# The attention norm's factors spread by a matrix product of ones with a diagonal; the multiply on VectorE; squares moved ahead, sums of logs behind

## The chip, the core and the metric

The kernel runs on one core of one Trainium2 chip. A core has five engines that each work through their own instructions in order: TensorE (PE, matrix products into the eight banks of PSUM), VectorE (DVE), ScalarE (ACT), GpSimd (POOL) and SyncE (SP), which issues most of the transfers (DMAs) between DRAM and the on-chip memory SBUF. Engines wait for each other through semaphores. The metric is the device time of one execution in microseconds (us); lower is better.

## The reference, cut to what matters

Two layers over 512 tokens of width 1024: a mixer (forgetting attention in layer 0, a gated short convolution in layer 1), a squared-ReLU MLP and a gated embedding, each between RMS norms. The change lies in the first norm and in the projections of the attention:

```python
def rmsnorm(x, g):
    xf = x.astype(jnp.float32)
    y = xf * lax.rsqrt(jnp.mean(xf * xf, axis=-1, keepdims=True) + RMS_EPS)
    return (y * g.astype(jnp.float32)).astype(x.dtype)

hn = rmsnorm(x, g[0])
proj = hn @ w_in                              # q, k, v and a forget logit for each head
f_logit = (proj[..., 3 * D:] + b_f).astype(jnp.float32)
log_f = jax.nn.log_sigmoid(f_logit)
c = lax.cumsum(log_f, axis=1).transpose(0, 2, 1)
s = s + cb[..., :, None] - c[..., None, :]    # in each block of queries, before the softmax
```

Each token has one factor `r = rsqrt(mean(x*x) + eps)`. Each attention score gets a difference of running sums of the logs.

## The kernel before

**Numbers.** Each operand of a product is split in two parts, `hi` (cast by ScalarE, L276 or L285) and `lo` (the rest, by VectorE, L277 or L287), and `mm3` (L266 to L272) makes three products out of them. The weights pass through the same split, after they landed in one of 14 buffers `raw`; the gain `g` goes into the weights.

**Tokens and the two ways of the norm.** The tokens are four blocks of 128, `t` = 0 to 3. The input is also there transposed, channels on partitions, in two pages for each block (`raw_x[t][n]`, `xT` in the trace). The value projection comes in three chunks of columns. Chunk 0 (256 values and the 16 forget logits) and chunk 1 (512 values) are multiplied with the transposed input *without* the norm, and `r`, a number for each token and thus for each partition of the result, is applied to the result (`keep_values`, L491: `logit` at L496, ScalarE's `v` at L512, VectorE's at L517). Chunk 2 (256 values) and all `q`, `k` need the normed input, `hT`, whose tokens run along the free dimension. For that `r` must stand on all partitions as a row.

**The row of factors.** `mean_squares` (L701) sums the squares of a block on ScalarE and VectorE, `inverse` (L708) raises to -1/2 on GpSimd: `rs[t]`, one number for each partition. `rows_of` (L716) writes these 128 numbers to DRAM (`r_T`, L717) and reads them back broadcast to all partitions (`r_row`, L718), both on SP's queue. `normed_x` (L722) multiplies each page `xT` by that row on GpSimd (L726) and splits it into `hTh`, `hTl` (L277).

**The logs.** `logs` (L419) makes `log_sigmoid` of the logits of all blocks, with `logf` (L436) as its last step, split into `lf_h`, `lf_l`. `sums_of_logs` (L441) multiplies them with a triangle of ones (`ps_c`, L445), copies the bank (`c_T`, L450), makes `neg_c` (L454) and writes it to DRAM (L458). `bias` (L556) reads `neg_c` back, broadcast (`pr`, `prr`, `prl`, L568). `project` (L528) makes `q` and `k` of two heads; copies of `kh`, `kl` to the other half of the partitions go as transfers on SP (L553). `scores` (L574) multiplies them (`sc`, L581, L582) and adds the bias.

**What sets the order.** From L731 on, until the squares and chunk 0 are done, instructions stand on each engine as the code is written. Behind that, a scheduler places each engine's instructions by its own model of the times; a change there moves rows. SP's transfers use eight semaphores in turn, so each waits for the eighth before it; a weight load also waits until its `raw` buffer has been split.

Of the kernel before, what the change touches and what calls it, by code (L numbers as in the profile page):

```python
# [8 lines left out]
F32 = mybir.dt.float32  # L9
F32R = mybir.dt.float32r  # L10
AF = mybir.ActivationFunctionType
ALU = mybir.AluOpType
# [3 lines left out]
P = 128  # L16
# [5 lines left out]
KT = D // P  # L22
NB = S // P
# [6 lines left out]
RAWS = 14  # L30
# [38 lines left out]
def trunk(ctx: ExitStack, tc, x, xT, pT, g, gT, wv, wqk, bf, wo, wci, wcq, cw, wco, wup, wdn, wpp, wpg, out):  # L69
    nc = tc.nc  # L70
# [7 lines left out]
    dram = pool("dram", 1, space=DRAM)  # L78

    def page(name, dtype=F32):  # L80
        return pages.tile([P, S], dtype, tag="pg", name=name)

    def bank(name):
        return psum.tile([P, S], F32, tag="ps", name=name)
# [4 lines left out]
    ident = consts.tile([P, P], F32, tag="ident", name="ident")  # L89
# [322 lines left out]
    def attention(hT, raw_x, first_x, b_f, work, by_hand):  # L412
# [47 lines left out]
        turned, rs = {}, {}  # L460
# [237 lines left out]
        name = "n0"  # L698
        E = mybir.EngineType

        def mean_squares(t):  # L701
            half = lambda n: first_x[t][n][:, :S]
            q = squares(half(0), f"{name}_q0_{t}"), products(half(1), f"{name}_q1_{t}")
            v = stat(f"{name}_v{t}")
            nc.vector.tensor_tensor(out=v, in0=q[0], in1=q[1], op=ALU.add)
            return v

        def inverse(t, v):  # L708
            r = stat(f"{name}_r{t}")
            nc.gpsimd.tensor_tensor(out=r, in0=v, in1=neg_half, op=ALU.pow)  # L710
            return r

        r_T = dram.tile([NB, P], F32, tag="r_T", name="r_T")
        r_row = page("r_row")

        def rows_of(t):  # L716
            nc.sync.dma_start(r_T[t : t + 1, :].rearrange("o p -> p o"), rs[t])  # L717
            nc.sync.dma_start(  # L718
                r_row[:, t * P : (t + 1) * P], r_T[t : t + 1, :].partition_broadcast(P)
            )  # L720

        def normed_x(t):  # L722
            for n in range(2):
                h = raw_x[t][n][:, :S].rearrange("p (j c) -> p j c", j=4)
                r = r_row[:, t * P : (t + 1) * P].unsqueeze(1).to_broadcast([P, 4, P])
                nc.gpsimd.tensor_tensor(out=h, in0=h, in1=r, op=ALU.mult)  # L726
                to = lambda u: u[:, 4 * n : 4 * n + 4, t * P : (t + 1) * P]
                split(to(hT.hi), to(hT.lo), h)

        banks_v = [bank(f"v0_{t}") for t in range(NB)]  # L730
        with tc.manual_schedule(engines={E.PE, E.DVE, E.Activation, E.Pool}):  # L731
            work(9)
            split_x(0, 0)
            prepare(4)
            part(banks_v[0], 0, 0)
            split_x(0, 1)
            split_x(1, 0)
            part(banks_v[1], 1, 0)
            prepare(KT)
            part(banks_v[0], 0, 1)  # L740
            split_x(1, 1)
            part(banks_v[1], 1, 1)
            for t in (2, 3):
                for n in range(2):
                    split_x(t, n)
                    part(banks_v[t], t, n)
            for t in range(2):
                rs[t] = inverse(t, mean_squares(t))
                prepare(KT + 2 * t + 2)
            prepare(2 * KT)  # L750
            for t in range(2):
                keep_values(0, t, banks_v[t])
            for t in (2, 3):
                rs[t] = inverse(t, mean_squares(t))
                keep_values(0, t, banks_v[t])
        for t in range(NB):
            rows_of(t)
        tri = page("tri", F32R)
        ones = page("ones")
        nc.gpsimd.memset(ones[:, :S], 1.0)  # L760
# [5 lines left out]
        logs()  # L766
        for t in range(NB):
            values(1, t)
            normed_x(t)
            if t == 2:  # L770
                sums_of_logs(tri)
        bias(0)
        bias(1)
        for t in range(NB):
# [522 lines left out]
```

## Time and profile before

| | |
|---|---|
| median of three runs | 1241.15 us (1239.37 to 1241.65) |
| the profiled execution | 1239.36 us |
| its span, first to last instruction | 1237.6 us |
| busy in the span | PE 98%, VectorE 76%, ScalarE 56%, GpSimd 54% |
| DRAM traffic over the span | 118 GB/s |

Rows of the waits name who waited, for whom, the us in total, the number of waits and the longest. Rows of the timelines give start, length, engine, line, operation, output <- inputs, shapes, and in brackets the idle time before and what ended it; `x4` are four instructions merged in one row. A product of PE is issued when the one before it has streamed, so the distance of starts counts, not the length that is shown. SPq rows are issues of transfers, not their landing.

### The profile page before, as it was taken

Reading aid. Unit: us, or ns where it says so; the run is one execution under the profiler, and the core shown is the slowest. Engines: PE = TensorE matmul, PEld = TensorE weight load, DVE = VectorE, ACT = ScalarE, POOL = GpSimd, SP = SyncE. Lnnn points to the kernel's source line nnn. Section 1 sums busy time; section 2 is a strip of 40 time slices with the busy share of each in tenths; the row PEclk is TensorE's granted clock in tenths of the full one; section 3 lists DMA queues with packets and bytes.
Section 4 is the critical chain, followed back from the end, with each engine's and each line's share of the span. In section 5 each row is a group of like instructions: output and inputs, shape, how many; then the busy total and the mean of one; then the engine's idle time right before and its main releaser. Section 6 shows DMA issues by size and latency. Waiting matters only on the chain.

```text
span 1237.6 us, 18749 instructions
## 1 busy us (share of the span) xinstructions
PE 1208.8 (98%) x6167; PEld 1028.7 (83%) x6167; DVE 935.5 (76%) x1466; ACT 690.0 (56%) x1465; POOL 668.8 (54%) x620
## 2 busy tenths in 40 slices
PE   9589999999999999999999999999999999999997
PEld 7478888788888888888889999989888888888886
DVE  6677888776786778769867798867776887669873
ACT  5646787656745634564467443455756345635551
POOL 0426666426776877776213155415678777778310
PEclk9799999999999999999999999999999999999999
DMA  9364656261442244228332233443322442235501
GB/s 309 102 180 146 167 152 160 88 226 52 136 130 68 78 134 136 86 69 272 119 103 66 63 102 103 145 146 111 115 73 85 137 135 88 60 127 161 180 6 62
DMA packets 88465, 151.09 MB, mean 122 GB/s; under 512 B 10992, under 2 KB 19232, under 8 KB 88368
## 3 DMA queue, kind: packets, MB, share of 16 engines
q1 hardware_dynamic: 87792, 149.37, 38.9%
q8 instruction: 48, 0.79, 0.3%
q10 hardware_dynamic: 576, 0.53, 0.1%
q14 instruction: 49, 0.40, 0.1%
HBM read 139.29 MB, written 6.38 MB: 118 GB/s over the span
## 4 chain that ended last, share of the span: by engine, by line
PE 85%; DMA 5%; DVE 4%; issue 2%; ACT 2%; POOL 1%; SPq 0%; POOLq 0%; DVEq 0%; ACTq 0%
PE up L270 9%; PE up L269 9%; PE up L268 9%; PE dn L268 8%; PE dn L269 8%; PE dn L270 8%; PE qk L270 2%; PE qk L269 2%; PE qk L268 2%; PE pg L269 2%; PE pg L268 2%; PE pg L270 2%; DMA raw<-in_wqk 2%; PE pT L597 1%; PE co L269 1%
## 5 line engine op out<-in xcount | busy, mean ns | idle before, releaser
L277 DVE TENSOR_TENSOR wl<-raw,wh 128x512 fp32r<-128x512 f32 x346 | 349.2, 1054 | 14.3 <-ACT wh L276 13.5
L269 PE MATMUL up<-hTh,wl 128*128 128x512 f32 (+1 forms) x576 | 210.2, 365 | 0.0
L270 PE MATMUL up<-hTl,wh 128*128 128x512 f32 (+1 forms) x576 | 209.7, 366 | 0.1
L268 PE MATMUL up<-hTh,wh 128*128 128x512 f32 (+1 forms) x576 | 208.7, 366 | 0.0
L276 ACT CAST wh<-raw 128x512 fp32r<-128x512 f32 x346 | 189.4, 625 | 4.5 <-DVE xd L373 4.4
L949 ACT ACTIVATE r<-up 128x512 f32<-128x512 f32 (+1 forms) x72 | 39.4, 548 | 201.9 <-PE up L270 160.0
L277 POOL TENSOR_TENSOR wl<-dn_T,wh 128x512 fp32r<-128x512 f32 x96 | 132.2, 1410 | 30.1 <-ACT wh L276 30.1
L168 POOL TENSOR_TENSOR dn_T<-raw,raw 128x512 f32<-128x512 f32 x56 | 86.1, 1550 | 70.8 <-DMA raw<-in_wdn 55.5
L268 PEld LDWEIGHTS up<-hTh,wh 128*128 128x128 f32 x576 | 108.6, 189 | 17.6
L269 PEld LDWEIGHTS up<-hTh,wl 128*128 128x128 f32 x576 | 108.6, 189 | 17.5
L270 PEld LDWEIGHTS up<-hTl,wh 128*128 128x128 f32 x576 | 108.3, 189 | 17.7 <-DVE hTl L277 0.3
L995 DVE TENSOR_TENSOR acc<-dn,acc 128x512 f32<-128x512 f32 x168 | 107.5, 680 | 13.9 <-PE dn L270 13.9
L168 POOL TENSOR_TENSOR dn_T<-raw,dn_T 128x512 f32<-128x512 f32 x56 | 92.9, 1658 | 2.2
L276 ACT CAST wh<-dn_T 128x512 fp32r<-128x512 f32 x112 | 61.4, 617 | 11.0 <-POOL dn_T L168 11.0
L277 DVE TENSOR_TENSOR A12l<-q,A12h 128x512 fp32r<-128x512 f32 x28 | 22.5, 802 | 52.9 <-ACT A12h L276 52.9
L1009 POOL TENSOR_TENSOR acc<-acc,acc 128x512 f32<-128x512 f32 x28 | 46.9, 1709 | 9.9 <-DVE acc L995 9.9
L268 PE MATMUL qk<-hTh,wh 128*128 128x512 f32 x128 | 51.1, 400 | 0.0
L269 PE MATMUL qk<-hTh,wl 128*128 128x512 f32 x128 | 51.1, 399 | 0.0
L270 PE MATMUL qk<-hTl,wh 128*128 128x512 f32 x128 | 51.0, 398 | 0.0
L269 PE MATMUL pg<-wh,hTl 128*128 128x512 f32 x128 | 50.5, 394 | 0.0
L287 DVE SCALAR_TENSOR_TENSOR wl<-raw,first_g,wh 128x256 fp32r<-128x256 f32 (+2 forms) x88 | 46.1, 571 | 5.7 <-ACT wh L285 5.4
L268 PE MATMUL pg<-wh,hTh 128*128 128x512 f32 x128 | 50.4, 394 | 0.0
(409 smaller groups left out, 3310.3 us busy)
## 6 DMA issues: line engine op xcount, KB each, us to landing
raw<-in_wup SPq DMA_DIRECT2D x128, 256.0 KB, 3.0
raw<-in_wdn SPq DMA_DIRECT2D x128, 256.0 KB, 2.8
raw<-in_wcq SPq DMA_DIRECT2D x36, 256.0 KB, 2.8
raw<-in_wqk SPq DMA_DIRECT2D x32, 256.0 KB, 5.5
raw<-in_wpg SPq DMA_DIRECT2D x32, 256.0 KB, 4.4
g<-in_g SPq DMA_DIRECT2D x22, 256.0 KB, 5.9
prl<-neg_c SPq DMA_DIRECT2D x16, 256.0 KB, 6.2
raw<-in_wo SPq DMA_DIRECT2D x16, 256.0 KB, 4.8
```

The source lines that it names most:

```text
L168: ins = nc.gpsimd.tensor_tensor(out=B[name], in0=B[a], in1=B[b], op=op)
L268: nc.tensor.matmul(ps, a.hi, b.hi, start=start, stop=False)
L269: nc.tensor.matmul(ps, a.lo, b.hi, start=False, stop=False)
L270: nc.tensor.matmul(ps, a.hi, b.lo, start=False, stop=stop)
L276: nc.scalar.copy(hi, src)
L277: return eng.tensor_tensor(out=lo, in0=src, in1=hi.bitcast(F32), op=ALU.subtract)
L287: eng.scalar_tensor_tensor(out=lo[:, c], in0=src[:, c], scalar=first_g[:, k : k + 1], in1=hi[:, c].bitcast(F32), op0=ALU.mult, op1=ALU.sub ...
L597: nc.tensor.transpose(ps[:, b * P : (b + 1) * P], probs[h][b][:, j * P : (j + 1) * P], ident)
L949: nc.scalar.activation(r[:, :n], ps[:, :n], AF.Relu)
L995: ins = nc.vector.tensor_tensor(out=a, in0=banks[s], in1=a, op=ALU.add)
L1009: nc.gpsimd.tensor_tensor(out=a, in0=a, in1=acc[i, s][:, :S], op=ALU.add)
```

## The change

- The round trip through DRAM goes. `rows_of` makes a diagonal matrix of the factors on GpSimd (`r_d`, 128 x 128) and multiplies a matrix of ones with it on PE, so that a quarter of one PSUM bank, `r_rows`, holds the row on all partitions.
- `normed_x` multiplies on VectorE, from that bank.
- The squares of blocks 2 and 3 are taken before the last two weights of chunk 1 and before chunk 0's results are kept.
- In the loop over the blocks of chunk 1 the rows come in pairs, `normed_x` lags one block, and `sums_of_logs` stands behind the loop.

```diff
-        r_T = dram.tile([NB, P], F32, tag="r_T", name="r_T")
-        r_row = page("r_row")
+        all_ones = page("all_ones")
+        nc.gpsimd.memset(all_ones[:, :P], 1.0)
+        r_rows = []
 
         def rows_of(t):
-            nc.sync.dma_start(r_T[t : t + 1, :].rearrange("o p -> p o"), rs[t])
-            nc.sync.dma_start(
-                r_row[:, t * P : (t + 1) * P], r_T[t : t + 1, :].partition_broadcast(P)
+            if not r_rows:
+                r_rows.append(bank("r_rows"))
+            d = page(f"r_d{t}")
+            nc.gpsimd.tensor_scalar(
+                out=d[:, :P], in0=ident, scalar1=rs[t], scalar2=None, op0=ALU.mult
+            )
+            nc.tensor.matmul(
+                r_rows[0][:, t * P : (t + 1) * P], all_ones[:, :P], d[:, :P],
+                start=True, stop=True,
             )
 
         def normed_x(t):
             for n in range(2):
                 h = raw_x[t][n][:, :S].rearrange("p (j c) -> p j c", j=4)
-                r = r_row[:, t * P : (t + 1) * P].unsqueeze(1).to_broadcast([P, 4, P])
-                nc.gpsimd.tensor_tensor(out=h, in0=h, in1=r, op=ALU.mult)
+                r = r_rows[0][:, t * P : (t + 1) * P].unsqueeze(1).to_broadcast([P, 4, P])
+                nc.vector.tensor_tensor(out=h, in0=h, in1=r, op=ALU.mult)
                 to = lambda u: u[:, 4 * n : 4 * n + 4, t * P : (t + 1) * P]
                 split(to(hT.hi), to(hT.lo), h)
...
                 prepare(KT + 2 * t + 2)
-            prepare(2 * KT)
-            for t in range(2):
-                keep_values(0, t, banks_v[t])
+            prepare(RAWS)
             for t in (2, 3):
                 rs[t] = inverse(t, mean_squares(t))
+            prepare(2 * KT)
+            for t in range(NB):
                 keep_values(0, t, banks_v[t])
-        for t in range(NB):
-            rows_of(t)
...
         for t in range(NB):
             values(1, t)
-            normed_x(t)
-            if t == 2:
-                sums_of_logs(tri)
+            if t in (0, 2):
+                rows_of(t)
+                rows_of(t + 1)
+            if t:
+                normed_x(t - 1)
+        sums_of_logs(tri)
+        normed_x(3)
```

Where the instructions stand now, at three places. Lines of the changed kernel are up to nine higher behind the diff; L733 is the multiply of `normed_x`, L724 the product with the diagonal.

VectorE at the end of the logs (`wl` are weight halves, `f_l` and `logf` the logs). Before:

```order
L287 SCALAR_TENSOR_TENSOR wl_479<-raw_480,first_g,wh_478 128x256
L434 TENSOR_TENSOR f_l<-f_l,f_r 128x64
L287 SCALAR_TENSOR_TENSOR wl_479<-raw_480,first_g,wh_478 128x256
L277 TENSOR_TENSOR hTl<-xT_0_90,hTh 128x4x128
L436 SCALAR_TENSOR_TENSOR logf<-logit,f_l 128x64
L287 SCALAR_TENSOR_TENSOR wl_490<-raw_491,first_g,wh_489 128x256 x2
```

Now:

```order
L287 SCALAR_TENSOR_TENSOR wl_471<-raw_472,first_g,wh_470 128x256 x2
L434 TENSOR_TENSOR f_l<-f_l,f_r 128x64
L287 SCALAR_TENSOR_TENSOR wl_482<-raw_483,first_g,wh_481 128x256 x2
L436 SCALAR_TENSOR_TENSOR logf<-logit,f_l 128x64
L287 SCALAR_TENSOR_TENSOR wl_493<-raw_494,first_g,wh_492 128x256 x2
L287 SCALAR_TENSOR_TENSOR wl_504<-raw_505,first_g,wh_503 128x256 x2
```

No half of `hT` stands ahead of `logf` any more; the first one comes 12 rows behind it.

VectorE from the copy of the running sums, `c_T`, to `neg_c`. Before:

```order
L277 TENSOR_TENSOR hTl<-xT_0_96,hTh 128x4x128
L450 COPY c_T<-ps_c 16x512
L517 SCALAR_TENSOR_TENSOR v_0_555<-v_0_466,n_r_344,v_0_555 128x2x64 x2
L517 SCALAR_TENSOR_TENSOR v_1_556<-v_0_466,n_r_344,v_1_556 128x2x64 x2
L517 SCALAR_TENSOR_TENSOR v_0_596<-v_1_571,n_r_361,v_0_596 128x2x64 x2
L517 SCALAR_TENSOR_TENSOR v_1_597<-v_1_571,n_r_361,v_1_597 128x2x64 x2
L454 TENSOR_SCALAR neg_c_664<-c_T 16x128
```

Now:

```order
L733 TENSOR_TENSOR xT_1_97<-xT_1_97,r_rows 128x512
L517 SCALAR_TENSOR_TENSOR v_0_677<-v_3_652,n_r_395,v_0_677 128x2x64 x2
L517 SCALAR_TENSOR_TENSOR v_1_678<-v_3_652,n_r_395,v_1_678 128x2x64 x2
L450 COPY c_T<-ps_c 16x512
L277 TENSOR_TENSOR hTl<-xT_0_92,hTh 128x4x128
L277 TENSOR_TENSOR hTl<-xT_1_93,hTh 128x4x128
L277 TENSOR_TENSOR hTl<-xT_0_94,hTh 128x4x128
L277 TENSOR_TENSOR hTl<-xT_1_95,hTh 128x4x128
L277 TENSOR_TENSOR hTl<-xT_0_96,hTh 128x4x128
L277 TENSOR_TENSOR hTl<-xT_1_97,hTh 128x4x128
L454 TENSOR_SCALAR neg_c_704<-c_T 16x128
```

All eight multiplies, all `v` of chunk 1 and all halves of `hT` now stand ahead of `neg_c`. Between `logf` and `c_T` VectorE's order is: the rest of the weight halves, four `v` (block 0), two multiplies, `hTl`, four `v` (block 1), `hTl`, four `v` (block 2), six multiplies, four `v` (block 3).

PE around the sums of logs, `ps_c` (L268 to L270 are products of chunk 1, `v_3` that of block 3). Before:

```order
L269 MATMUL v_2_612<-wh_385,xl_1_290 128x512
L270 MATMUL v_2_612<-wl_386,xh_1_289 128x512
L445 MATMUL ps_c<-tri,lf_h 16x512
L268 MATMUL v_3_676<-wh_346,xh_0_305 128x512
L269 MATMUL v_3_676<-wh_346,xl_0_306 128x512
```

Now:

```order
L269 MATMUL v_3_652<-wh_403,xl_1_322 128x512
L724 MATMUL r_rows<-r_d_640,all_ones 128x128
L270 MATMUL v_3_652<-wl_404,xh_1_321 128x512
L445 MATMUL ps_c<-tri,lf_h 16x512
L724 MATMUL r_rows<-r_d_643,all_ones 128x128
L445 MATMUL ps_c<-tri,lf_l 16x512
```

The sums come behind all of chunk 1, and the rows of blocks 2 and 3 between them. In the built program the product for block 2 waits until VectorE's multiplies of block 0 have read the bank. Before, chunk 1 of blocks 0 and 1 was interleaved on PE; now block 0 stands alone in front. Behind PE's products of chunk 2 for block 0, five products that need `hT` of all blocks follow, and then the rest of blocks 1 to 3. On SP the eight transfers of the row are gone, and the order of the others is as before. Among the 64 steps of the attention many rows of PE and some of the other engines moved by a few places; behind the attention the order is the same.

## The prediction

> **What bounds the kernel now.** I read the page's engine totals first, then TensorE's waits in two stretches, then the chain of waits, and last the timelines of the engines around the largest wait.
>
> ```profile
> PE 1208.8 (98%) x6167; PEld 1028.7 (83%) x6167; DVE 935.5 (76%) x1466; ACT 690.0 (56%) x1465; POOL 668.8 (54%) x620
> ```
>
> TensorE (PE) is busy for 98% of the span, so a gain must come out of its 29 us of gaps. Its longest wait from 15 to 92 us, and the longest behind `sc` from 92 to 300 us:
>
> ```profile
> PE ps_c L445 <- ACT lf_h L276: 15.1, 1, 15.1
> ...
> PE o L270 <- DVE wl L277: 0.3, 1, 0.3
> ```
>
> With the 2.7 and 1.0 us in the timeline below, 18.8 us of the gaps stand before 92 us; behind that PE waits for next to nothing, so whatever brings the score products (`sc`) at 91.7 us forward brings the end forward by as much. The gaps in PE's timeline:
>
> ```profile
> 35.75 0.39 PE L270 MATMUL v<-wl,xh 128*128 128x512 f32 x1
> 51.22 0.61 PE L445 MATMUL ps_c<-tri,lf_h 128*16 128x512 f32 x1 [15.09 <-ACT lf_h L276]
> 51.63 0.63 PE L268 MATMUL v<-wh,xh 128*128 128x512 f32 x1
> 52.05 0.63 PE L269 MATMUL v<-wh,xl 128*128 128x512 f32 x1
> ...
> 59.17 0.33 PE L268 MATMUL v<-wh,hTh 128*128 128x256 f32 x1
> ...
> 71.20 0.40 PE L268 MATMUL qk<-hTh,wh 128*128 128x512 f32 x1
> ...
> 87.32 0.39 PE L270 MATMUL qk<-hTl,wh 128*128 128x512 f32 x1
> 90.41 0.30 PE L581 MATMUL sc<-kh,qs 128*128 128x128 f32 x1 [2.70 <-DMA kh<-kh]
> 91.72 0.47 PE L582 MATMUL sc<-kl,qs 128*128 128x128 f32 x1 [1.01 <-DMA kl<-kl]
> ```
>
> The chain of waits says what `lf_h` waited for:
>
> ```profile
> 27.54 10.23 DMA raw<-in_wqk
> 37.78 8.35 DMA r_row<-r_T
> 46.28 1.27 POOL xT L726
> 47.57 0.63 ACT hTh L276
> 49.23 0.34 DVE logf L436
> ```
>
> The logs do not need the norm's rows. But ScalarE (ACT) and VectorE (DVE) take work in order, and `hTh` and `hTl`, which wait for the round trip of `r` through DRAM (back at 46.1 us), stand ahead of `logf`. The second gate is a transfer: `neg_c` leaves VectorE, is written, read back and broadcast, and the `kh`, `kl` copies queue behind those and weight loads on SyncE (SP):
>
> ```profile
> 66.84 1.25 DVE L454 TENSOR_SCALAR neg_c<-c_T 16x128 f32<-16x128 f32 x4
> ...
> 67.13 1.73 SPq L458 DMA_DIRECT2D neg_c<-neg_c  x4
> ...
> 82.70 0.53 SPq L553 DMA_DIRECT2D kh<-kh  x1
> ...
> 85.65 0.47 SPq L553 DMA_DIRECT2D kl<-kl  x1
> ```
>
> SP issues within 0.3 us of `neg_c`; `sc` follows the start of `neg_c` by 91.72 - 66.84 = 24.9 us. That is how long this chain takes, and its order on SP is unchanged.
>
> **The change part by part.** *Removed:* four `r_T` writes and four `r_row` reads on SP, and eight multiplies on GpSimd (POOL), which took 1.42 us each and slowed VectorE meanwhile:
>
> ```profile
> 46.28 11.37 POOL L726 TENSOR_TENSOR xT<-xT,r_row 128x512 f32<-128x512 f32 x8 [11.25 <-DMA r_row<-r_T]
> ...
> 53.29 1.77 DVE L277 TENSOR_TENSOR hTl<-xT,hTh 128x512 fp32r<-128x512 f32 x1
> 54.98 2.95 DVE L287 SCALAR_TENSOR_TENSOR wl<-raw,first_g,wh 128x256 fp32r<-128x256 f32 x2
> ...
> 59.38 0.68 DVE L277 TENSOR_TENSOR hTl<-xT,hTh 128x512 fp32r<-128x512 f32 x1
> 59.98 0.87 DVE L287 SCALAR_TENSOR_TENSOR wl<-raw,first_g,wh 128x256 fp32r<-128x256 f32 x2
> ```
>
> A pair of `wl` takes 2.95 us beside POOL's multiplies and 0.87 after them.
>
> With the DRAM trip gone nothing holds `logf` up; what sets `neg_c` is VectorE's own queue. I lay that queue out from 26.31 us, up to which it issues what it did before (the moved squares of tokens 2 and 3 fall into its idle 2.41 us):
>
> ```profile
> 24.97 1.42 DVE L287 SCALAR_TENSOR_TENSOR wl<-raw,first_g,wh 128x512 fp32r<-128x512 f32 x2 [2.41 <-ACT wh L285]
> 26.31 0.23 DVE L496 SCALAR_TENSOR_TENSOR logit<-v,n_r,b_f 128x16 f32<-128x16 f32 x1
> ...
> 27.75 0.22 DVE L496 SCALAR_TENSOR_TENSOR logit<-v,n_r,b_f 128x16 f32<-128x16 f32 x1
> ...
> 33.89 0.23 DVE L496 SCALAR_TENSOR_TENSOR logit<-v,n_r,b_f 128x16 f32<-128x16 f32 x1 [0.66 <-POOL n_r L710]
> ...
> 36.36 0.36 DVE L765 CAST tri<-ones 128x512 fp32r<-128x512 f32 x1
> ...
> 64.77 2.14 DVE L517 SCALAR_TENSOR_TENSOR v<-v,n_r,v 128x128 fp32r<-128x128 f32 x8
> ...
> 70.69 3.24 DVE L287 SCALAR_TENSOR_TENSOR wl<-raw,first_g,wh 128x256 fp32r<-128x256 f32 x8
> ```
>
> 1. *Squares sooner.* Four rounds `logit`, `v` now follow each other at 27.75 - 26.31 = 1.44 us; the fourth `logit` stands at 26.31 + 3 x 1.44 = 30.63 instead of 33.89. To the end of `tri` it is 36.36 + 0.31 - 33.89 = 2.8 us as before: 33.4.
> 2. *Logs and weight halves.* ScalarE's `wh` for the next weight sits behind the table load and sets the pace once:
>
> ```profile
> 35.13 0.26 ACT L425 ACTIVATE f_e<-f_n 128x64 f32<-128x64 f32 x1 [0.35 <-DVE f_n L424]
> 35.41 1.28 ACT L427 ACT_TABLE_LOAD   x1
> ...
> 36.86 1.69 ACT L285 ACTIVATE wh<-raw,first_g 128x256 fp32r<-128x256 f32 x4
> ...
> 56.87 3.17 ACT L512 ACTIVATE v<-v,n_r 128x128 fp32r<-128x128 f32 x12
> ```
>
>    `f_e` at 30.63 + 1.24 = 31.9, a `wh` pair 0.85 (1.69 / 2), table load and logarithm to 34.5, a `wh` pair to 35.3, its `wl` done at 35.7. Then six pairs at 2 x 0.405 (3.24 / 8) and three small ones of 0.13: 40.95. ScalarE keeps pace, ends its last `wh` at 40.3 (35.3 + 6 x 0.81 + 0.13) and then does four `v` at 0.265 (3.17 / 12), to 41.4; VectorE's four at 0.27 (2.14 / 8) end at 42.45.
> 3. *The multiplies, now on VectorE from PSUM.* No row has this one. Lower bound: `hTl`, 59.98 - 59.38 = 0.60 us. Upper: POOL's 1.42. I take 0.61, because the nearest row is VectorE's addition of a bank to a page of the same size:
>
> ```profile
> L995 DVE TENSOR_TENSOR acc<-dn,acc 128x512 f32<-128x512 f32 x168 | 107.5, 680 | 13.9 <-PE dn L270 13.9
> ```
>
>    Two multiplies to 43.65, `hTl` 0.60 behind ScalarE's `hTh` to 44.3, four `v` behind ScalarE's to 45.8, `hTl` to 46.4, four `v` to 47.45, six multiplies to 51.1, four `v` to 52.2.
> 4. *Sums of logs later.* `c_T`, 0.60, and six `hTl`, 3.60, stand ahead of `neg_c`: 52.2 + 4.2 = **56.4**, against 66.84. Had the sums stayed ahead of the six `hTl`, 3.6 us more would be won here.
>
> So the gate moves by 66.84 - 56.4 = 10.4 us and `sc` from 91.72 to 56.4 + 24.9 = 81.3. The other parts hide below it:
>
> - *Four small products on PE.* Their price lies between 0.06 us (`ps_c` with 128 columns, 59.17 - 59.11 below) and 0.43, the half-clock pitch of a 512-column product; I take 0.1. PE is early by then, so this costs nothing. The third one waits until VectorE has read the bank for tokens 0 (43.65), and `ps_c` and the `hT` products stand behind it:
>
> ```profile
> 59.11 0.22 PE L445 MATMUL ps_c<-tri,lf_l 128*16 128x128 f32 x1
> ```
>
> - *PE's own arrival.* It now takes the chunk of tokens 0 alone and waits for the last weight half at 26.3 (before, it filled that time with tokens 1): 26.5, then 72 products at 0.227 us give 42.9; the third small product 43.65; `ps_c` 44.9; `hT` products of tokens 0 until 48.0 (the second `hTl` at 46.4 + 12 x 0.12); tokens 1 wait for `hTl` at 52.2 + 0.6 + 0.6 = 53.4, a new gap of about 5 us. 71 products at 0.12 (71.20 - 59.17 over 96) end at 61.9, 68 `qk` products at 0.227 at **77.4**. That is 3.9 us ahead of `sc`; without the transfer's cover this would be the gate.
> - *Half clock.* After the 15.1 us gap products stand 52.05 - 51.63 = 0.42 us apart instead of 0.23. Should the new gap do the same, the 20-odd products behind it cost up to 2.2 us: 79.6, still before 81.3. [...]
> - *Four diagonals on POOL*, next to the last `wl` and the `logit` rounds. Nearest rows: the `wl` pair above went from 0.87 to 2.95 us, so one overlapped `wl` may lose up to 1 us; none if the idle parts of the rounds take them. I take 0 and keep 1 us in the range. [...]
>
> **Sum.** The profiled execution took 1239.36 us (span 1237.6); less 10.4 that is 1229.0. The median of the three runs, 1241.15, lies 1.8 above the profiled one; less 10.4: **1230.75**, say 1230.7.
>
> **Rivals.**
>
> *A. Transfers shorten and PE sets the end.* If the 24.9 us from `neg_c` shrink (no `r_row` trip in front, other landings), `sc` comes at PE's 77.4 to 79.6, another 1.7 to 3.9 us: 1226.8 to 1229.0. Against it: at 67 us the trip had long ended, and the bytes behind are the same.
>
> *B. The multiply from PSUM is slow.* At POOL's 1.42 us, eight of them add 8 x 0.81 = 6.5 us ahead of `neg_c`: 1237.2. Against it: the 168 additions at 680 ns.
>
> *C. The wait only moves.* If SP's weight loads and not `neg_c` set `kl`, `sc` stays near 91.7: 1241, no change. Against it: SP issued 0.3 us behind `neg_c`.
>
> *D. Slower: the attention steps fall behind.* The scheduler also reorders products of PE among the 64 score steps after 92 us, and VectorE, which feeds them, is nearly full there:
>
> ```profile
> 210.00:230.00 20.00, 19.43 (x105) 15.08 (x105) 19.00 (x58) 17.75 (x48) 16.14 (x20) 1.00 0.45 99
> ```
>
>    (PE 19.43, VectorE 19.00 of 20 us.) A wait of the size seen there, 0.3 us, in each of 64 steps costs 19.2 us: 1249.9. It outweighs the gain from 10.4 / 64 = 0.16 us per step. Against it: such a wait is rare now, and the rows move by a few places.
>
> **How the numbers follow.** Forecast 0.65, A 0.14, B 0.10, C 0.05, D 0.06. The forecast's own range, with the diagonals' 1 us and 1.5 us for the layout, is 1228.5 to 1233.5. The range, 1226 to 1237.5, takes in A and B and leaves out C and D. About 0.2%, 2.5 us, is what a measurement of this kernel can tell from no change: faster than 1238.7 are the forecast, A and B, 0.89; C gives same, 0.05; D slower, 0.06.
>
> **What the changed profile would show.** No wait of 15 us for `lf_h`; `logf` near 36 us; `neg_c` on VectorE at 56 (later than 58: B, if the multiplies are above 0.7 us; otherwise my layout is off); PE's gaps of about 5 us at `hTl` of tokens 1 and 2 to 4 us at `kh` and `kl`; `sc` near 81, 25 us behind `neg_c` (less: A; much more: C). A sum of PE waits above 3 us between `sc` and 300 us shows D. I am wrong about the path if `sc` moves by another amount than `neg_c`.

## The result, and the profile after

| | before | changed |
|---|---|---|
| median of five runs | 1240.84 us | 1230.68 us |
| range | 1239.37 to 1241.65 | 1229.76 to 1232.38 |
| profiled execution (span) | 1239.36 (1237.6) | 1231.56 (1229.8) |

The ratio of the times is 0.9923, 95% interval 0.9908 to 0.9937: the change takes 9.5 us off, between 7.8 and 11.4.

The engine totals of the changed kernel:

```profile
PE 1213.2 (99%) x6175; PEld 1030.7 (84%) x6175; DVE 932.0 (76%) x1474; ACT 690.2 (56%) x1465; POOL 657.1 (53%) x617
```

TensorE's waits of the changed kernel between 15 and 92 us (who waited, for whom, us in total, times, longest):

```profile
PE v L268 <- ACT wh L285: 1.7, 1, 1.7
PE v L268 <- ACT hTh L276: 1.6, 2, 0.8
PE sc L581 <- DMA kh<-kh: 1.3, 1, 1.3
PE sc L582 <- DMA kl<-kl: 1.0, 1, 1.0
PE v L269 <- DVE hTl L277: 0.6, 1, 0.6
```

The wait of 15.1 us for `lf_h` is gone. What is left are small waits, and `sc` still waits for its two transfers. From 92 to 300 us the same view has nothing above 0.4 us:

```profile
PE o L268 <- ACT wh L276: 0.4, 1, 0.4
PE pT L597 <- DVE pl L602: 0.4, 1, 0.4
PE sc L581 <- DVE oT L626: 0.2, 1, 0.2
```

VectorE's timeline of the changed kernel (start, length, line, operation, count), to be read against the steps of the prediction:

```profile
32.31 0.22 DVE L496 SCALAR_TENSOR_TENSOR logit<-v,n_r,b_f 128x16 f32<-128x16 f32 x1
...
37.87 0.22 DVE L436 SCALAR_TENSOR_TENSOR logf<-logit,f_l 128x64 f32<-128x64 f32 x1
...
45.95 1.13 DVE L517 SCALAR_TENSOR_TENSOR v<-v,n_r,v 128x128 fp32r<-128x128 f32 x4 [0.35 <-PE v L270]
...
48.63 3.67 DVE L733 TENSOR_TENSOR xT<-xT,r_rows 128x512 f32<-128x512 f32 x6
...
53.85 3.68 DVE L277 TENSOR_TENSOR hTl<-xT,hTh 128x512 fp32r<-128x512 f32 x6
57.46 1.26 DVE L454 TENSOR_SCALAR neg_c<-c_T 16x128 f32<-16x128 f32 x4
```

`logf` follows the logits without a long wait, six of the eight multiplies from PSUM take 3.67 / 6 = 0.61 us each, and `neg_c` stands at 57.46 us, 9.4 sooner than before. TensorE's timeline around the gaps:

```profile
51.21 0.38 PE L268 MATMUL v<-wh,hTh 128*128 128x256 f32 x1 [0.81 <-ACT hTh L276]
52.40 0.39 PE L268 MATMUL v<-wh,hTh 128*128 128x256 f32 x1 [0.81 <-ACT hTh L276]
...
54.57 0.58 PE L269 MATMUL v<-wh,hTl 128*128 128x256 f32 x1 [0.60 <-DVE hTl L277]
...
82.23 0.30 PE L581 MATMUL sc<-kh,qs 128*128 128x128 f32 x1 [1.26 <-DMA kh<-kh]
83.52 0.33 PE L582 MATMUL sc<-kl,qs 128*128 128x128 f32 x1 [1.00 <-DMA kl<-kl]
```

`sc`, at 91.72 us before, is at 83.52: 8.2 us sooner, and the span is 7.8 us shorter. From the second product of `sc` to the end of the span it is 1146.3 us (1145.9 before). TensorE itself would have been at `sc` at 82.23 - 1.26 = 81.0 us.

One execution of the experiments below stands apart: the profiled one of a4 took 4489.05 us where its other four took 1226.19 to 1228.50, so that its trace is not read, it counts in a4's median alone (1226.8 us without it) and not in its ratio.

### The profile page after: what moved, and what is told of

It is laid out like the page before. It is cut to its first block, busy times and chain, and to the rows that moved or that the text cites. A ratio compares the mean times of both kernels' runs of the same rounds, so it can differ in the third digit from the quotient of the medians.

```text
span 1229.8 us, 18755 instructions
## 1 busy us (share of the span) xinstructions
PE 1213.2 (99%) x6175; PEld 1030.7 (84%) x6175; DVE 932.0 (76%) x1474; ACT 690.2 (56%) x1465; POOL 657.1 (53%) x617
## 4 chain that ended last, share of the span: by engine, by line
PE 88%; DMA 4%; issue 2%; DVE 2%; ACT 2%; POOL 2%; SPq 0%; POOLq 0%; DVEq 0%; ACTq 0%
PE up L268 9%; PE up L269 9%; PE up L270 9%; PE dn L268 8%; PE dn L269 8%; PE dn L270 8%; PE qk L270 2%; PE qk L269 2%; PE pg L268 2%; PE qk L268 2%; PE pg L270 2%; PE pg L269 2%; PE pT L597 1%; PE co L268 1%; PE co L269 1%
## 5 line engine op out<-in xcount | busy, mean ns | idle before, releaser
L270 PE MATMUL up<-hTl,wh 128*128 128x512 f32 (+1 forms) x576 | 209.6, 365 | 0.0
L268 PE MATMUL up<-hTh,wh 128*128 128x512 f32 (+1 forms) x576 | 208.7, 366 | 0.0
L268 PEld LDWEIGHTS up<-hTh,wh 128*128 128x128 f32 x576 | 108.6, 189 | 17.6
L270 PEld LDWEIGHTS up<-hTl,wh 128*128 128x128 f32 x576 | 108.3, 189 | 17.6
L270 PE MATMUL qk<-hTl,wh 128*128 128x512 f32 x128 | 51.1, 400 | 0.0
L268 PE MATMUL qk<-hTh,wh 128*128 128x512 f32 x128 | 50.7, 396 | 0.0
L268 PE MATMUL pg<-wh,hTh 128*128 128x512 f32 x128 | 50.4, 394 | 0.0
L277 DVE TENSOR_TENSOR A11l<-q,A11h 128x256 fp32r<-128x256 f32 x28 | 22.6, 807 | 36.5 <-ACT A11h L276 36.5
```

The lines of the kernel that those rows point to most:

```text
L268: nc.tensor.matmul(ps, a.hi, b.hi, start=start, stop=False)
L270: nc.tensor.matmul(ps, a.hi, b.lo, start=False, stop=stop)
L277: return eng.tensor_tensor(out=lo, in0=src, in1=hi.bitcast(F32), op=ALU.subtract)
```

## The experiments

Each time is the median of a run's repetitions, with its ratio to the kernel before in the same session. In the row of a4 and b4, the time and the ratio are a4's and the rest is b4's, one execution of the same kernel (1225.81 us). That kernel's own median was between 1238.53 and 1240.84 us in the sessions, so two variants of different sessions are compared by their ratios. "neg_c" is the start of the first `neg_c` on VectorE and "sc" that of the second product of `sc` (which needs `kl`), both in the profiled execution; "wait" is TensorE's at the first two products of `sc`, "clock" its mean in the 3 us behind.

| run | us | ratio (95%) | neg_c | sc | neg_c to sc | wait | clock | sc to end of span |
|---|---|---|---|---|---|---|---|---|
| before | 1240.84 | 1 | 66.84 | 91.72 | 24.9 | 3.7 | 0.50 | 1145.9 |
| changed | 1230.68 | 0.9923 (0.9908 to 0.9937) | 57.46 | 83.52 | 26.1 | 2.3 | 0.57 | 1146.3 |
| a1 trip kept | 1236.66 | 0.9981 (0.9969 to 0.9993) | 67.66 | 91.76 | 24.1 | 1.8 | 1.00 | 1144.4 |
| a2 logs ahead | 1234.55 | 0.9961 (0.9950 to 0.9972) | 63.69 | 88.19 | 24.5 | 3.3 | 0.60 | 1145.9 |
| a3 neg_c late | 1233.75 | 0.9951 (0.9936 to 0.9966) | 61.65 | 86.50 | 24.9 | 7.6 | 0.50 | 1146.6 |
| a4, b4 sums in the middle | 1227.12 | 0.9901 (0.9876 to 0.9926) | 48.21 | 79.76 | 31.6 | 0 | 1.00 | 1144.3 |
| b1 rows only | 1236.06 | 0.9973 (0.9963 to 0.9983) | 58.56 | 90.16 | 31.6 | 0 | 1.00 | 1143.8 |
| b2 squares late | 1239.42 | 0.9997 (0.9986 to 1.0007) | 64.31 | 90.23 | 25.9 | 4.4 | 0.50 | 1146.7 |
| b3 rows first | 1228.23 | 0.9910 (0.9889 to 0.9931) | 50.48 | 82.04 | 31.6 | 0 | 1.00 | 1143.7 |
| c1 woven | 1220.79 | 0.9860 (0.9842 to 0.9877) | 46.80 | 74.45 | 27.7 | 0 | 1.00 | 1144.6 |
| c2 own queue | 1230.11 | 0.9929 (0.9907 to 0.9951) | 57.58 | 82.67 | 25.1 | 3.7 | 0.53 | 1146.6 |
| c3 GpSimd multiplies | 1227.22 | 0.9914 (0.9895 to 0.9933) | 53.11 | 80.52 | 27.4 | 0 | 1.00 | 1145.0 |
| d1 one bias later | 1224.81 | 0.9885 (0.9868 to 0.9901) | 55.89 | 77.84 | 22.0 | 0.6 | 1.00 | 1145.1 |

The last column carries the study: wherever `sc` lies, from 74 to 92 us, the rest takes 1143.7 to 1146.7 us. All but 3 us is decided ahead of `sc`.

### What of the gain is the row's way, and what is order?

**a1.** The kernel before, with all moves of the change and the old trip through DRAM:

```diff
-            prepare(2 * KT)
-            for t in range(2):
-                keep_values(0, t, banks_v[t])
+            prepare(RAWS)
             for t in (2, 3):
                 rs[t] = inverse(t, mean_squares(t))
+            prepare(2 * KT)
+            for t in range(NB):
                 keep_values(0, t, banks_v[t])
...
-            normed_x(t)
-            if t == 2:
-                sums_of_logs(tri)
+            if t:
+                normed_x(t - 1)
+        sums_of_logs(tri)
+        normed_x(3)
```

> The kernel before with every move of the change in the written order (squares sooner, normed_x one block behind, sums behind the loop), but with the row still going through DRAM and GpSimd multiplying. Theory (the row's way, not the written order, gives the gain): the order on ACT and VectorE still has hTh and hTl ahead of logf, so TensorE again waits over 10 us for lf_h; r_T of blocks 2 and 3 goes out some us sooner, which takes at most 2 us off: 1238.5 to 1241. Rival (the moves alone do it): TensorE's long wait goes, neg_c stands near 57 us, 1230 to 1232.

Ratio 0.9981: the moves alone take 2.4 us off, between 0.9 and 3.8, where the theory had 2 at most. The profile shows TensorE's waits as the theory had them:

```profile
PE ps_c L445 <- ACT lf_h L276: 11.6, 1, 11.6
PE ps_c L445 <- DVE lf_l L277: 4.9, 1, 4.9
```

The wait for the logs is 16.5 us, and `sc` is where it was (91.76). The 2.4 us are not in the gate; the span behind `sc` is 1.4 us shorter (1145.9 to 1144.4; the last section has a likely reason).

**a2.** The kernel before and one rule more: no `hTh` ahead of `lf_h` on ACT, no `hTl` ahead of `lf_l` on VectorE. The round trip and GpSimd's multiplies stay.

```diff
...
-                split(to(hT.hi), to(hT.lo), h)
+                behind(nc.scalar.copy(to(hT.hi), h), log_ins[0])
+                behind(nc.vector.tensor_tensor(
+                    out=to(hT.lo), in0=h, in1=to(hT.hi).bitcast(F32), op=ALU.subtract
+                ), log_ins[1])
```

(`log_ins` are the two operations that make `lf_h` and `lf_l`)

> The kernel before, with one thing added: hTh may not stand ahead of lf_h on ACT, nor hTl ahead of lf_l on VectorE. The round trip and GpSimd's multiplies stay. Theory (the trip cost 15 us only because logf was queued behind it): the 15 us wait of TensorE goes, neg_c stands at 58 to 60 us behind the seventh hTl (GpSimd's multiplies still end at 57 us), sc at 83.5 to 86, 1231 to 1234. Rival (the latency of the trip itself is what costs): TensorE waits for hTh or hTl instead for most of the 15 us, sc stays within 3 us of 91.7, 1238 to 1241.

The theory in part: ratio 0.9961, 4.8 us off (3.5 to 6.2), about half of the change's gain with the trip still there. The time lies 0.6 us above the theory's range, and TensorE's waits did not go altogether:

```profile
PE v L269 <- DVE hTl L734: 5.3, 2, 2.8
PE ps_c L450 <- ACT lf_h L441: 5.1, 1, 5.1
```

Of the 15.1 us for `lf_h` 10 were thus the price of what stood in front of `logf`; 5.1 stayed, and 5.3 of waits for `hTl` are new. VectorE's timeline says what kept `neg_c` from more:

```profile
53.25 3.43 DVE L734 TENSOR_TENSOR hTl<-xT,hTh 128x512 fp32r<-128x512 f32 x2
...
63.69 1.25 DVE L459 TENSOR_SCALAR neg_c<-c_T 16x128 f32<-16x128 f32 x4
```

Two `hTl` take 3.43 us, waits between them included, where in the changed kernel six take 3.68: GpSimd's multiplies run beside them, and `neg_c` comes at 63.7 instead of the 58 to 60 expected, `sc` at 88.2 instead of 83.5 to 86.

**b1.** The product with the diagonal and the multiply on VectorE alone; squares, `normed_x` and sums of logs stay as they were written before:

```diff
+        for t in range(NB):
+            rows_of(t)
         for t in range(NB):
             values(1, t)
-            if t in (0, 2):
-                rows_of(t)
-                rows_of(t + 1)
-            if t:
-                normed_x(t - 1)
-        sums_of_logs(tri)
-        normed_x(3)
+            normed_x(t)
+            if t == 2:
+                sums_of_logs(tri)
```

(against the changed kernel, with its squares back at the old place)

> The kernel before with the product of ones and the diagonal and the multiply on VectorE alone: squares, normed_x and sums of logs stay written where they were. Theory (the row's way brings the gain and the moves little): VectorE issues all eight multiplies in a row, then the hTl, so neg_c comes at about 57 us as in the changed kernel (the squares cost 1.6 us, but only two rounds of v stand ahead), sc at 82 to 84, 1229 to 1231.5. Rival (the moves are part of the gain): neg_c 2 us or more later than 57.5, 1233 or more.

The theory missed: 1236.06. It is the rival's time, but not its way: `neg_c` came near the 57 us expected (58.56), and `sc` waited for neither transfer: TensorE itself was late. Its timeline:

```profile
36.24 0.80 PE L724 MATMUL r_rows<-r_d,all_ones 128*128 128x128 f32 x2 [16.04 <-POOL r_d L721]
```

and GpSimd's of the same run:

```profile
33.86 0.55 POOL L710 TENSOR_TENSOR n_r<-n_v,neg_half 128x1 f32<-128x1 f32 x1 [2.52 <-DVE n_v L705]
...
35.56 2.69 POOL L721 TENSOR_SCALAR r_d<-ident,n_r 128x128 f32<-128x128 f32 x4
```

The scheduler put the product at the head of chunk 1 on TensorE. Its diagonal stands on GpSimd behind the factor of block 3, and that factor comes from the late squares. One wait of 15 us on TensorE became one of 16.

**b2.** The changed kernel, with the squares alone at their old place:

```diff
-            prepare(RAWS)
+            prepare(2 * KT)
+            for t in range(2):
+                keep_values(0, t, banks_v[t])
             for t in (2, 3):
                 rs[t] = inverse(t, mean_squares(t))
-            prepare(2 * KT)
-            for t in range(NB):
                 keep_values(0, t, banks_v[t])
```

> The changed kernel with the squares of blocks 2 and 3 back behind the results of blocks 0 and 1. Theory: VectorE's queue to neg_c is gapless, so the fourth logit comes at 33.9 instead of 32.3 us, neg_c at 59.0 instead of 57.5, sc 1.6 us later, 1232.3. Rival (VectorE's idle time behind the logs takes it in): neg_c and sc as in the changed kernel, 1230.7.

Both theories missed: 1239.42, no gain that can be told from none is left (0.9986 to 1.0007). TensorE's first row product and VectorE's multiplies:

```profile
35.74 0.79 PE L724 MATMUL r_rows<-r_d,all_ones 128*128 128x128 f32 x2 [8.72 <-POOL r_d L721]
```

```profile
55.47 3.68 DVE L733 TENSOR_TENSOR xT<-xT,r_rows 128x512 f32<-128x512 f32 x6 [3.82 <-PE r_rows L724]
...
64.31 1.26 DVE L454 TENSOR_SCALAR neg_c<-c_T 16x128 f32<-16x128 f32 x4
```

TensorE waits 8.7 us for the diagonal at 27 us, so chunk 1 ends later, and the rows of blocks 2 and 3, which stand behind it on TensorE, hold VectorE for 3.8 us more. `neg_c` is 6.9 us later than in the changed kernel, not 1.6. The parts of the change do not add: moves 2.4 us, the row's way alone 3.3 (b1), the row's way with the new order but late squares 0.4 (not clear of zero), all together 9.5.

### Does neg_c set sc?

**a3.** Six idle operations between `c_T` and `neg_c`:

```diff
             nc.vector.tensor_copy(c_T[:H, :S], ps_c[:H, :])
+            for b in range(6):
+                nc.vector.tensor_tensor(out=c_T[:H, :S], in0=c_T[:H, :S], in1=c_T[:H, :S], op=ALU.max)
```

> The changed kernel with six idle operations of VectorE (max of c_T with itself, 0.6 us each) between c_T and neg_c: only neg_c and what VectorE does behind it come 3.6 us later. Theory (neg_c sets sc by a chain of transfers of 25 to 26 us): neg_c at 61.1, the second product of sc at 87.1 instead of 83.5, 1234.3. Rival (the weight loads behind TensorE's chunk 2 set sc, since the chain of waits runs through them): those loads are released at 66 us as before, sc moves by less than 1 us, 1231 to 1231.7.

Near the theory, which had 3.6 us for each: `neg_c` 4.2 us later (the six took 4.24), `sc` 3.0, the time 3.5 by the ratios (0.9951 to 0.9923). At `sc` TensorE waited for the transfers alone:

```profile
85.39 0.45 PE L583 MATMUL sc<-kh,qs 128*128 128x128 f32 x1 [6.92 <-DMA kh<-kh]
86.50 0.47 PE L584 MATMUL sc<-kl,qs 128*128 128x128 f32 x1 [0.67 <-DMA kl<-kl]
```

**a4 and b4.** The sums written behind block 2's values, as before the change:

```diff
             if t in (0, 2):
                 rows_of(t)
                 rows_of(t + 1)
+            if t == 2:
+                sums_of_logs(tri)
             if t:
                 normed_x(t - 1)
-        sums_of_logs(tri)
         normed_x(3)
```

> The changed kernel with the sums of logs written behind block 2's values instead of behind the loop (where they stood before the change): c_T and neg_c now stand ahead of the last six multiplies and hTl on VectorE. neg_c near 49 us instead of 57.5; hTl of block 1 comes some 1.2 us later (56.4), and TensorE's arrival at sc from 81.0 to 82.2. Theory: the transfers no longer set sc, TensorE's arrival does: sc's second product near 82.3 without a wait for kh or kl, 1229.4. Rival (weight loads behind chunk 2 set it): sc 1.2 us later than in the changed kernel, 84.7, with the waits for kh and kl still there, 1231.9.

The time, 1227.12, is below both expectations; b4, the same kernel once more, gave the trace.

> The changed kernel with the sums of logs behind block 2's values once more, for its trace: neg_c near 49 us, sc's second product at 80 (1227.1 less 1230.7, from 83.5), set by TensorE's own arrival (theory: no wait for kh or kl above 0.5 us) or by the weight loads (rival: waits for kh and kl of 1 us each as in the changed kernel).

```profile
48.21 1.26 DVE L454 TENSOR_SCALAR neg_c<-c_T 16x128 f32<-16x128 f32 x4
...
79.70 0.22 PE L581 MATMUL sc<-kh,qs 128*128 128x128 f32 x1
79.76 0.28 PE L582 MATMUL sc<-kl,qs 128*128 128x128 f32 x1
```

No wait stands before either product: with `neg_c` at 48.21 the transfers are in time and TensorE's own arrival, 79.7, is the gate. "Sums of logs later" thus looks like a part of the change that costs: with the sums sooner `sc` is 3.8 us ahead (83.52 to 79.76). That rests on the traces; the ratios lie 2.7 us apart, but their intervals overlap.

**c2.** The copies of `kh` and `kl` of the first two heads on ACT's queue:

```diff
-                            nc.sync.dma_start(h[b, :S].bitcast(F32), h[a, :S].bitcast(F32))
+                            (nc.scalar if i == 0 else nc.sync).dma_start(
+                                h[b, :S].bitcast(F32), h[a, :S].bitcast(F32))
```

> The changed kernel with the four copies of kh and kl of the first two heads issued by ACT on its own queue instead of SP's. Theory (the 25 us from neg_c to sc are the queue of broadcasts and weight loads that the copies stand behind): sc follows TensorE's arrival, 79 to 82, and not the 83.5 of the changed kernel, 1227 to 1229. Rival (the DMA engines are shared, and the copies wait for them on any queue): sc at 83 to 84, 1230 to 1231.5.

The rival's time: 1230.11; `sc` at 82.67 lies between the two expectations. The issues, on ACT's queue:

```profile
74.44 0.51 ACTq L553 DMA_DIRECT2D kh<-kh  x1
75.76 0.47 ACTq L553 DMA_DIRECT2D kl<-kl  x1
```

and in the changed kernel, on SP's:

```profile
74.52 0.53 SPq L553 DMA_DIRECT2D kh<-kh  x1
...
77.15 0.47 SPq L553 DMA_DIRECT2D kl<-kl  x1
```

Another queue brought the issue of `kh` forward by nothing and that of `kl` by 1.4 us: in the built program each transfer waits for the eighth before it, whatever its queue, and for the first `kh` that is the last of the eight broadcasts. (`kh` itself was there at 68.9 us, and GpSimd could work on that broadcast, `prl`, from 74.5.) Once issued, `kl` still took until 82.67, 6.9 us for 128 KB, as against 83.52 - 77.15 = 6.4 on SP. A queue of its own buys nothing here. The two causes, the shared turn of semaphores and the shared engines, were not separated.

**d1.** Three of the eight broadcasts, 512 of 1280 KB, behind these copies:

```diff
         bias(0)
-        bias(1)
         for t in range(NB):
             values(2, t)
         for _ in project(0):
             pass
+        bias(1)
```

> The changed kernel with bias(1) written behind project(0): three of the eight broadcast reads of neg_c (512 of 1280 KB) are issued behind the copies of kh and kl of the first two heads instead of ahead of them and of the weight loads. Theory (kh and kl wait for the bytes ahead of them on 16 shared DMA engines: the eight broadcasts take 14 us from first issue to last landing in both traces): everything behind lands some 5 us sooner, TensorE's arrival at 78.5 to 81 sets sc, its waits for kh and kl shrink below 0.5 us, 1225.5 to 1228. Rival (the weight loads wait for their buffers, released from 66 us on, and set kh and kl): sc at 82 to 83.5 with waits of 1 us as before, 1229.5 to 1231. A third outcome: the second head's bias comes late, a new wait of VectorE or TensorE for it between 84 and 100 us gives it back.

The theory's way, and slightly sooner than its range: 1224.81. SP issued the first `kh` at 68.77, 5.7 us sooner (1.6 of them because `neg_c` was that much sooner in this execution), and TensorE's waits nearly end:

```profile
76.96 0.30 PE L581 MATMUL sc<-kh,qs 128*128 128x128 f32 x1
77.84 0.33 PE L582 MATMUL sc<-kl,qs 128*128 128x128 f32 x1 [0.59 <-DMA kl<-kl]
```

From `neg_c` to `sc` it is 22.0 us instead of 24 to 26. The second head's bias, now late, brought no new wait of TensorE at the scores. So the transfers ahead of `kh` and `kl` are a part of the 25 us: from `neg_c` to the issue of `kh` it is 12.9 us instead of 17.1, and the changed kernel gains 4.7 us by the ratios (0.9923 to 0.9885). How the rest divides is not shown.

### What the multiply on VectorE is worth

**c3.** The rows from TensorE, copied by ACT to a page, and the multiplies back on GpSimd:

```diff
+        r_row = page("r_row")
...
-                r = r_rows[0][:, t * P : (t + 1) * P].unsqueeze(1).to_broadcast([P, 4, P])
-                nc.vector.tensor_tensor(out=h, in0=h, in1=r, op=ALU.mult)
+                r = r_row[:, t * P : (t + 1) * P].unsqueeze(1).to_broadcast([P, 4, P])
+                nc.gpsimd.tensor_tensor(out=h, in0=h, in1=r, op=ALU.mult)
...
                 rows_of(t + 1)
+                nc.scalar.copy(r_row[:, t * P : (t + 2) * P], r_rows[0][:, t * P : (t + 2) * P])
```

> The changed kernel with the eight multiplies back on GpSimd: ACT copies each pair of rows from the bank to an SBUF page, and GpSimd multiplies by that; the product of ones with the diagonal and all the moves stay. Theory (VectorE's queue sets neg_c, and takes 4.9 us of multiplies off; beside GpSimd a hTl takes up to 1.4 us instead of 0.6): neg_c at 52 to 55.5 instead of 57.5, sc at 79 to 82, 1226 to 1229. Rival (the multiply on VectorE is what brought the gain, GpSimd's slow ones and the slowed VectorE beside them give it back): neg_c at 59 or later, 1232 or more.

The theory's numbers: 1227.22, `neg_c` at 53.11, `sc` at 80.52, 3.0 us ahead of the changed kernel. By the ratios it is 1.1 us faster, and the intervals overlap, so no difference is shown: the gain can be had without the multiply on VectorE. What the multiply alone costs the run does not say, for the scheduler moved rows as well. VectorE has eight multiplies less (4.9 us), but four of its eight `hTl`, all of which stood ahead of `neg_c`, now stand behind it (4 x 0.61 = 2.4 us). Against that stand what GpSimd's multiplies do to their neighbours, and a wait of TensorE for the diagonals of blocks 2 and 3, which now stand behind four of these multiplies:

```profile
41.77 2.40 DVE L517 SCALAR_TENSOR_TENSOR v<-v,n_r,v 128x128 fp32r<-128x128 f32 x8 [0.32 <-ACT v L512]
44.09 5.25 DVE L277 TENSOR_TENSOR hTl<-xT,hTh 128x512 fp32r<-128x512 f32 x4
...
53.11 2.85 DVE L454 TENSOR_SCALAR neg_c<-c_T 16x128 f32<-16x128 f32 x4
55.89 1.88 DVE L277 TENSOR_TENSOR hTl<-xT,hTh 128x512 fp32r<-128x512 f32 x3
```

```profile
42.07 5.89 POOL L734 TENSOR_TENSOR xT<-xT,r_row 128x512 f32<-128x512 f32 x4 [13.66 <-ACT r_row L778]
```

```profile
49.03 0.49 PE L725 MATMUL r_rows<-r_d,all_ones 128*128 128x128 f32 x2 [3.58 <-POOL r_d L722]
```

Four `hTl` take 5.25 us beside GpSimd instead of 2.4.

### Two versions written to beat both

**b3.** All rows and multiplies first, sums behind block 2's values, `hTl` of blocks 1 to 3 held behind `neg_c`:

```diff
+        for t in range(NB):
+            rows_of(t)
         for t in range(NB):
             values(1, t)
-            if t in (0, 2):
-                rows_of(t)
-                rows_of(t + 1)
-            if t:
-                normed_x(t - 1)
-        sums_of_logs(tri)
-        normed_x(3)
+            if t == 2:
+                sums_of_logs(tri)
+                normed_x(1)
+            if t != 1:
+                normed_x(t)
...
-                split(to(hT.hi), to(hT.lo), h)
+                low = split(to(hT.hi), to(hT.lo), h)
+                if done_sums and t:
+                    behind(low, done_sums[0])
```

(`done_sums[0]` is the last `neg_c`)

> The changed kernel with all four rows and all eight multiplies first, the sums of logs written behind block 2's values, and hTl of blocks 1 to 3 held behind neg_c on VectorE. Theory: neg_c near 50 us, so the transfers are in by 76; TensorE finds hTl of block 0 at 48 and of block 1 at 52 us, loses 2 us there instead of 4.5, and arrives at 76 to 77; sc 77, 1224.2 (1223 to 1226). Rival (weight loads or buffers of weights hold it, because the splits of the weights now all stand ahead): sc above 80, 1227 or more.

`neg_c` came as expected (50.48) but `sc` only at 82.04, without a wait there. Neither weights nor buffers held it, though; it was once more the first row product, at the head of chunk 1, TensorE's only wait up to `sc`:

```profile
27.24 0.80 PE L727 MATMUL r_rows<-r_d,all_ones 128*128 128x128 f32 x2 [7.78 <-POOL r_d L724]
```

Its ratio, 0.9910, has an interval that overlaps the changed kernel's, so a gain over that is not shown.

**c1.** The rows behind chunk 1 of block 0 on TensorE, and VectorE's order woven by hand, so that the halves of a block are there when TensorE needs them:

```diff
         for t in range(NB):
             values(1, t)
-            if t in (0, 2):
-                rows_of(t)
-                rows_of(t + 1)
-            if t:
-                normed_x(t - 1)
-        sums_of_logs(tri)
-        normed_x(3)
+            if t == 0:
+                for u in range(NB):
+                    rows_of(u)
+            if t == 2:
+                sums_of_logs(tri)
+            normed_x(t)
+        dve = [*normed[0], *normed[1][:2], *sums, *normed[1][2:], *normed[2], *normed[3]]
+        for before_, ins in zip(dve, dve[1:]):
+            behind(ins, before_)
+        for t, low in late_v:
+            if t >= 0:
+                behind(low, dve[-1])
```

(`normed[t]` are a block's two multiplies and two `hTl`, `sums` are `c_T` and the four `neg_c`, `late_v` the `v` of chunk 1 on VectorE)

> The changed kernel with VectorE's order made by hand behind the weight halves: multiplies and hTl of block 0, multiplies of block 1, c_T and neg_c, hTl of block 1, then multiplies and hTl of blocks 2 and 3, and all v of chunk 1 last; the four rows stand together behind TensorE's chunk 1 of block 0, the sums of logs behind that of block 2. Theory (neg_c or TensorE's gaps, whichever ends last, set sc): neg_c at 45 to 47 us, transfers in by 72; hTl of each block is ready before TensorE needs it, so it loses nothing between chunk 1 and sc and arrives at 74 to 75.5; 1222 (1221 to 1224). Rival (weight loads of the projections, or banks that v holds, stop TensorE instead): waits of 3 us or more for wl or a bank between 47 and 75 us, 1225 or more.

1220.79, a little better than expected; the ratio 0.9860 stands 7.8 us below that of the changed kernel. TensorE's waits between 15 and 300 us, all of them:

```profile
PE v L268 <- ACT wh L285: 0.8, 1, 0.8
PE o L270 <- DVE wl L277: 0.3, 1, 0.3
PE ps_o L624 <- DVE nmx L588: 0.2, 1, 0.2
```

Behind 26 us TensorE has no wait left up to `sc` at 74.45. This is the version to take. d1's later bias was not tried with it; `sc` waits for no transfer there.

## Why the prediction was right

**The path was right.** The end moves with `sc`, and `sc` with `neg_c` as long as TensorE is there in time: shown by a3 (later), b4 (sooner, until TensorE is the gate) and the last column of the table. The prediction named a sign against it, `sc` moving by another amount than `neg_c`: they moved 8.2 and 9.4 us. The 1.2 us between them are of the size by which the chain from `neg_c` to `sc` differs between traces (next paragraph).

**The fit to 0.1 us is partly chance.** The gate was to move 10.4 us and `sc` to 81.3; in the profiled execution `neg_c` moved 9.4 and `sc` came at 83.5, 2.2 us late, and that execution took 1231.56 where the sum gave 1229.0. The medians lie 10.2 us apart, the profiled executions 7.8: before, the profiled one was the fastest of its five, in the changed kernel the second slowest. The interval of the gain, 7.8 to 11.4 us, holds both. The same order of VectorE has `neg_c` at 55.89 in d1 and 57.58 in c2, so an execution says this to about 1 us, and the chain from `neg_c` to `sc`, carried over as 24.9, was 26.1 here and 24.1 to 25.9 in a1, a2, a3, b2 and c2, where TensorE waited for `kl` too.

*Step 1, squares sooner.* The pace was right (27.97 to 32.31 is 3 x 1.447 us), the start was not: the first `logit` stood at 27.97, not 26.31, since the last weight half of chunk 1 came 1.3 us later (VectorE began it at 26.28 instead of 24.97) and the pair took 1.77 us instead of 1.42. What the step did not see is the squares' larger part: the diagonals need the factors of blocks 2 and 3, in GpSimd's order. Late squares would have cost not the 3.3 us of this step but 6.9 us at `neg_c` and the whole gain (b2).

*Step 2, logs and weight halves.* The last `wl` ended at 42.18 instead of 40.95, `logf` stood at 37.9 instead of 36: the late start, carried on.

*Step 3, the multiplies.* 0.61 us each, as taken. Rival B is out.

*Step 4, sums later.* `c_T`, six `hTl`, `neg_c` in that order, 0.60 + 3.6 us, and 57.46 at the end. The remark that sums ahead of the six `hTl` would win 3.6 us was borne out in kind: b4, whose sums stand ahead of the six multiplies as well, has `sc` 3.8 us sooner, limited by TensorE's own arrival.

*TensorE's arrival* is the term that was mis-sized: 77.4 to 79.6 forecast, 81.0 measured. The gap of 5 us came as three of 0.81, 0.81 and 0.60 us, because products of other blocks stand between, but the clock fell from 1.00 to 0.50 at the end of them and stayed there until 60 us. In a3, with gaps of 0.25, 0.81 and 0.86 us at the same place, the clock stayed at 1.00, and TensorE arrived at 85.39 - 6.92 = 78.5: from the last gap on it needed 24.0 us instead of 26.4, so the clock of 0.50 cost about 2.4 us, the difference of the two traces, where up to 2.2 were allowed for it. The rest is about the late start of step 1. It cost nothing, as forecast, since the transfers came later still.

*Rival A* did not happen in the changed kernel (2.3 us of waits at `kh` and `kl`), but d1 and b4 show that it was the next bound. *Rival C* fell with a3. *Rival D* is out: 1.0 us of waits from 92 to 300 us, below the 3 that were named for it.

*The diagonals on GpSimd* were taken at 0 to 1 us for VectorE and the products at 0.1 us for TensorE; that was about their price as work (a product shows as two instructions, `x2`, and held TensorE for 0.24 us at the first and 0.14 us at the second, by the distance of starts). Their wait, 8 to 16 us in b1, b2 and b3, was not in the sum, and need not have been in this order of TensorE, where the first product stands behind 24 others.

## What to carry to other kernels

An engine that works in order charges a late operand to everything behind it: look for what stands ahead of the operation that the waiting engine needs (here `hTh` and `hTl` ahead of `logf`, 10 of 15.1 us by a2), before removing the transfer that made it late; half of the gain was to be had so. Where an operand comes from a new engine, follow it to its own source: a product that waits for a diagonal is as bad as a transfer (TensorE's wait was 16.0 us in b1 and 15.1 before), and whether it does was decided by a move elsewhere in the program. When a gate has moved, ask at once which bound is next, how far, and what it costs to move both; here the next two bounds together were worth most of the change's gain again (7.8 us by c1, after 9.5).

## What the runs showed of the hardware

**Behind much the same short gaps the clock was 0.50 in one trace and 1.00 in another.** Two windows of the changed kernel, from 50 to 58 us (us in the window, then busy time of TensorE, its weight loads, VectorE, ScalarE and GpSimd with counts, TensorE's clock, DMA share, GB/s):

```profile
50.00:54.00 4.00, 2.36 (x10) 1.18 (x8) 4.00 (x10) 4.00 (x8) 0.00 (x0) 0.91 0.00 0
54.00:58.00 4.00, 3.43 (x16) 3.43 (x17) 4.00 (x9) 2.47 (x8) 0.00 (x0) 0.50 0.00 0
```

The same windows of a3, whose gaps there are 0.25, 0.81 and 0.86 us:

```profile
50.00:54.00 4.00, 2.56 (x14) 1.65 (x12) 4.00 (x10) 4.00 (x9) 0.00 (x0) 1.00 0.00 0
54.00:58.00 4.00, 3.51 (x29) 3.51 (x30) 4.00 (x7) 2.82 (x10) 0.00 (x0) 1.00 0.00 0
```

In the changed kernel no single gap was longer than 0.81 us, 2.2 us in all; in a3 they add to 1.9. What makes the clock fall is not shown: in a2 a gap of 2.5 us, ahead of 55.05 us, was followed by a clock of 0.50 and one of 2.8 us, ahead of 66.63 us, by 1.00. It matters at `sc`, as the table's columns show for these traces: where TensorE waited there for 2.3 us or more, in two pieces, the clock behind it was 0.50 to 0.60 and the rest of the span 1145.9 to 1146.7 us; where it waited 1.8 us or less, 1.00 and 1143.7 to 1145.1. The 3 us behind `sc` in the changed kernel and in b4:

```profile
83.60:86.60 3.00, 3.00 (x10) 2.63 (x11) 2.48 (x9) 0.99 (x3) 0.36 (x1) 0.57 0.29 68
```

```profile
79.80:82.80 3.00, 3.00 (x17) 2.59 (x16) 2.13 (x8) 2.92 (x6) 0.13 (x1) 1.00 0.97 282
```

At a clock of 0.57, 3 us do the work of 1.7, so some 1.3 us are lost (an estimate from the clock and from the kernel before, where products of 512 columns stood 0.42 us apart at a clock of 0.50 and 0.23 at 1.00; the products in the two windows are not the same ones). A wait of that size at that place was thus paid twice in these traces, once as a wait and once as clock. It fits the 1.4 us that a1, with its clock at 1.00 instead of 0.50 in these 3 us, was faster behind `sc`.

**Beside GpSimd's multiplies one operation of VectorE took twice as long, another about as long as without them.** In c3 `hTl`, with two inputs in SBUF, took 5.25 / 4 = 1.31 us beside GpSimd's multiplies instead of 0.61; `v`, which reads the bank, 2.40 / 8 = 0.30 instead of 1.13 / 4 = 0.28. Whether this comes from where the operands lie is not shown, since the two operations differ in kind and size as well. In the same trace it was also GpSimd that took longer: the three `hTl` at 55.89 us took 1.88 / 3 = 0.63 us each, while GpSimd's multiply beside them took 3.88 us, where its first took 1.29.
